# Seven-product pairs of a gated MLP: a raw buffer pool for one quarter of the weights, and matmuls held to the order in which the kernel writes them

## The chip, the cores and the metric

The kernel runs on one core of one Trainium2 chip. The metric is device time in microseconds (us): the median of several executions. A profile is one further execution, recorded by the hardware profiler; its span runs from the first to the last recorded instruction, and its own time is a little longer than its span. The engines are called PE (matrix multiply), PEld (its weight loads), DVE (vector), ACT (scalar), POOL (general) and SP (which here only issues transfers).

## The reference

One decoder layer over 512 tokens of width 1024, in float32: a combined input projection, block-sparse causal attention and a causal mean-pool mixer in parallel, gates, an output projection, a layer norm, and then a gated MLP with a causal width-3 convolution, followed by a second layer norm. The part that matters here is the MLP's input projection:

```python
a, u = jnp.split(h @ w_ffn_in[l], 2, axis=-1)     # h: (512, 1024), each half: (512, 2816)
a = causal_dwconv(a, conv_w[l], conv_b[l])
f = (jax.nn.gelu(a, approximate=False) * u) @ w_ffn_out[l]
h = layer_norm(ALPHA * h + f, ln2_g[l], ln2_b[l])
```

The 2816 columns of `a` and of `u` are cut into 22 tiles of 128; tile `f` of `a` and tile `f` of `u` make a pair.

## The kernel before

**Number format.** Each float32 operand is split into a rounded part (hi) and a remainder (lo), and a product is three matmuls: hi·hi, hi·lo, lo·hi (`mm3`, lines 182 to 186). For a weight chunk the split costs ACT a copy into `whi` (line 69) and then DVE a subtraction into `wlo` (line 70). A chunk is 128 x 1024 (512 KB) or, for the quarter called D, 128 x 512 (256 KB).

**Stages.** Input projection and attention, branch projections, output projection and first layer norm, MLP input, MLP output (itself done with seven products over a 2 x 2 blocking), second layer norm. All weights pass one list, `chunks`, in order. `weights(i)` runs the list ahead to chunk `i + LEAD` (LEAD is 3) and hands back chunk `i`; `fetch` loads a chunk into a raw buffer (`wraw`, 3 buffers) and splits it into one of 5 `whi` and one of 5 `wlo` buffers (RING).

**Seven-product pairs.** For `f` from 4 to 17 (`SEVEN`), the 2 x 2 scheme is used over the two halves of the reduction (`k1`, `k2`) and the two halves of the tokens (`t1`, `t2`), so that a pair needs seven products of 4 x 3 matmuls with 256 columns in place of eight. Four chunks stand for its weights: A (the `a` tile), X (a sum built in memory: a load of `u` by SP, line 131, on which POOL's accumulating transfer adds `a`, line 132), D (the second half of the `u` tile, loaded by itself) and Y, which is not loaded: two DVE additions make it from X's raw buffer and A's raw buffer (line 144), into a raw buffer of its own. `fetch_seven` (lines 134 to 151) does this; A, D and Y draw on the same three `wraw` buffers, and X has two `xraw` buffers in the pool `xu`. That pool stands where `hraw` (16 KB a partition) stood before. X's load is issued five chunks ahead (`AHEAD`).

`seven(f)` writes its products in this order, each by `s_mm`: A0 (first half of A), X0, then the previous pair's last product Y1 (kept in the list `pending`), Y0, A1, D0, X1. Three banks hold the results: `sa` receives A0, Y0, X1 and Y1 one after the other, `sb` receives X0 and D0, `sc` receives A1. Between them ACT and DVE read partial results out (lines 699 to 711). After Y1, `gated` (lines 621 to 630) does the convolution, the GELU and the product with `u`. In the profile a matmul's operands tell the product: `sa<-hT` is A0 or Y1, `sa<-nT` is Y0 or X1, `sb<-T` is X0 or D0, `sc<-hT` is A1.

**What sets the order.** The kernel is written as one sequence; the compiler's scheduler places each engine's instructions by a modelled timeline. An instruction whose operands the model takes as late is overtaken by a later-written one that it takes as ready. The resulting order of each engine is fixed in the program, and so is the assignment of buffers: a chunk takes a buffer that the model saw come free. On the chip each engine then works through its own list.

## Time and profile before

| what | value |
|---|---|
| runs shown | 651.03, 651.3, 653.6 us; median 651.3 |
| the profiled execution | 649.74 us, of it span 648.0 |
| PE busy | 635.7 us in 3586 matmuls |
| DVE, ACT, POOL busy | 449.5, 328.0, 111.6 us |
| bytes moved | 94.79 MB, mean 146 GB/s |
| granted clock of PE | 0.996 of full, mean |
| seven-product stage | 347.95 us (first A0) to about 500 us (last Y1), 1176 matmuls of 256 columns |

The 40-slice rows of the page give each engine's busy share in tenths. A matmul's recorded duration overlaps the next one's, so the distance from one matmul's start to the next is what tells of lost time: 0.12 us for 256 columns.

### The profile page before, as it was taken

The page shows a single profiled execution, that of the slowest core. Times are in us where ns is not written, and L with a number is a line of the kernel's source. Part 1 is how long each engine was busy: PE and PEld are TensorE (multiplying, and loading weights), DVE is VectorE, ACT ScalarE, POOL GpSimd, SP SyncE. Part 2 cuts the span into 40 slices and gives each one's busy share as a digit, 9 for nine tenths or more (in the row PEclk, how much of TensorE's full clock was granted, in tenths as well). Part 3 has the DMA queues.
Part 4 walks back from the last instruction along what each step waited for, and adds up shares of the span by engine and source line. Part 5 has one row for each costly group of instructions (what it writes and reads, how often), then busy time and mean ns, then how long its engine had stood idle before and what let it go on. Part 6 is the DMA issues. An engine that isn't in the chain of part 4 may idle for free.

```text
span 648.0 us, 9322 instructions
## 1 busy us (share of the span) xinstructions
PE 635.7 (98%) x3586; PEld 551.4 (85%) x3586; DVE 449.5 (69%) x666; ACT 328.0 (51%) x475; POOL 111.6 (17%) x153
## 2 busy tenths in 40 slices
PE   9999999999999999999999999999999999999994
PEld 6888787877888888888999999998998888888884
DVE  6466665564532576299667888787986859698596
ACT  6547556675522333215444556455665337465452
POOL 1605361211000123300010101010100201123302
PEclk9999999999999999999999999999999999999998
DMA  9643222212222227404056686677635895989905
GB/s 323 197 166 99 82 81 82 74 67 89 74 95 98 91 98 286 136 1 162 2 150 173 170 208 155 179 179 188 165 128 163 274 264 137 218 188 193 282 4 129
DMA packets 32540, 94.79 MB, mean 146 GB/s; under 512 B 3688, under 2 KB 3944, under 8 KB 32240
## 3 DMA queue, kind: packets, MB, share of 16 engines
q1 hardware_dynamic: 22832, 66.91, 30.4%
q0 software_dynamic: 9088, 26.24, 20.7%
q10 hardware_dynamic: 576, 1.05, 0.5%
q8 instruction: 28, 0.46, 0.3%
q14 instruction: 16, 0.13, 0.1%
HBM read 91.02 MB, written 3.17 MB: 145 GB/s over the span
## 4 chain that ended last, share of the span: by engine, by line
PE 91%; DVE 3%; POOL 2%; DMA 1%; ACT 1%; issue 1%; DVEq 0%; ACTq 0%; POOLq 0%
PE fi L186 5%; PE fi L184 5%; PE fi L185 5%; PE g L184 5%; PE g L186 4%; PE g L185 4%; PE sa L184 4%; PE sa L186 4%; PE sa L185 4%; PE v L285 3%; PE wo L186 2%; PE br L186 2%; PE br L184 2%; PE wo L184 2%; PE wo L185 2%; PE br L185 2%
## 5 line engine op out<-in xcount | busy, mean ns | idle before, releaser
L70 DVE TENSOR_TENSOR wlo<-wraw,whi 128x1024 fp32r<-128x1024 f32 (+1 forms) x119 | 144.1, 1214 | 59.2 <-ACT whi L69 57.7
L69 ACT ACTIVATE whi<-wraw 128x1024 fp32r<-128x1024 f32 (+1 forms) x118 | 117.2, 996 | 131.9 <-PE g L185 23.6
L186 PE MATMUL fi<-hT_hi,wlo 128*128 128x512 f32 (+1 forms) x168 | 56.7, 339 | 0.0
L185 PE MATMUL fi<-hT_lo,whi 128*128 128x512 f32 (+1 forms) x168 | 56.7, 339 | 0.0
L184 PE MATMUL fi<-hT_hi,whi 128*128 128x512 f32 (+1 forms) x168 | 56.4, 340 | 0.0
L184 PE MATMUL g<-xT_hi,whi 128*128 128x512 f32 x128 | 50.3, 393 | 0.0
L186 PE MATMUL g<-xT_hi,wlo 128*128 128x512 f32 x128 | 49.9, 390 | 0.0
L185 PE MATMUL g<-xT_lo,whi 128*128 128x512 f32 x128 | 49.8, 389 | 0.0
L132 POOL DMA_DIRECT2D xraw<-in_w_fi x14 | 17.0, 1215 | 183.7 <-DVE y L624 70.2
L69 ACT ACTIVATE whi<-tw 128x1024 fp32r<-128x1024 f32 (+1 forms) x30 | 29.4, 982 | 21.6 <-DMA tw<-in_w_fo 8.1
L70 DVE TENSOR_TENSOR wlo<-tw,whi 128x1024 fp32r<-128x1024 f32 (+1 forms) x30 | 33.3, 1127 | 8.4 <-ACT whi L69 8.4
L185 PEld LDWEIGHTS fi<-hT_lo,whi 128*128 128x128 f32 x168 | 31.9, 190 | 3.5
L186 PEld LDWEIGHTS fi<-hT_hi,wlo 128*128 128x128 f32 x168 | 31.9, 190 | 3.3
L184 PEld LDWEIGHTS fi<-hT_hi,whi 128*128 128x128 f32 x168 | 31.6, 190 | 3.3
L184 PE MATMUL sa<-hT_hi,whi 128*128 128x256 f32 x112 | 31.9, 285 | 2.0 <-ACT whi L69 1.9
L186 PE MATMUL sa<-hT_hi,wlo 128*128 128x256 f32 x112 | 31.7, 284 | 0.0
L185 PE MATMUL sa<-hT_lo,whi 128*128 128x256 f32 x112 | 31.6, 283 | 0.0
L184 PE MATMUL sb<-T_hi,whi 128*128 128x256 f32 x112 | 31.5, 282 | 0.0
L184 PE MATMUL sa<-nT_hi,whi 128*128 128x256 f32 x112 | 31.5, 281 | 0.0
L186 PE MATMUL sa<-nT_hi,wlo 128*128 128x256 f32 x112 | 31.3, 279 | 0.0
L185 PE MATMUL sa<-nT_lo,whi 128*128 128x256 f32 x112 | 31.3, 279 | 0.0
L185 PE MATMUL sb<-T_lo,whi 128*128 128x256 f32 x112 | 31.3, 279 | 0.0
(250 smaller groups left out, 1762.8 us busy)
## 6 DMA issues: line engine op xcount, KB each, us to landing
wraw<-in_w_fi SPq DMA_DIRECT2D x30, 512.0 KB, 3.6
wraw<-in_w_c SPq DMA_DIRECT2D x28, 512.0 KB, 3.4
tw<-in_w_fo POOLq DMA_DIRECT2D x20, 512.0 KB, 8.3
xraw<-in_w_fi SPq DMA_DIRECT2D x14, 512.0 KB, 4.9
xraw<-in_w_fi POOLq DMA_DIRECT2D x14, 512.0 KB, 5.7
wraw<-in_w_fo SPq DMA_DIRECT2D x10, 512.0 KB, 5.1
tw<-in_w_fo SPq DMA_DIRECT2D x10, 512.0 KB, 6.6
wraw<-in_w_br SPq DMA_DIRECT2D x8, 512.0 KB, 3.3
```

What stands on the lines that cost most here:

```text
L69: nc.scalar.activation(hi, src, AF.Copy)
L70: nc.vector.tensor_tensor(lo, src, hi.bitcast(F32), op=ALU.subtract)
L132: nc.gpsimd.dma_start(v, bass.AP(tensor=a.tensor, offset=a.offset, ap=[[pst, pn], [u.offset + S - a.offset, 2], [est, S]]), accum_op=ALU.add)
L184: nc.tensor.matmul(out_, wh, ah, start=start, stop=False, **kw)
L185: nc.tensor.matmul(out_, wh, al, start=False, stop=False, **kw)
L186: nc.tensor.matmul(out_, wl, ah, start=False, stop=stop, **kw)
L285: nc.tensor.matmul(bs[j], xs_[j][a], (wh, wl)[b], start=kt == 0 and n == 0, stop=False)
```

## The change

D gets raw buffers of its own: two tiles `draw` of 128 x 512 in the pool `xu`; `wraw`, still three buffers, serves A and Y alone in these pairs. The list `pending` is created early, since `fi_mm` now reads it. `mm3` takes a function `pin`, applied to each of its three matmuls. `s_mm` passes `tc.keep_in_program_order`, and `fi_mm` (the plain tiles) passes it while a Y1 is pending, which is so for one tile, the first after pair 17. That function adds a scheduling edge to the instruction written just before on the same engine: the pinned matmul is placed behind it. It adds no semaphore wait. All matmuls of the 14 pairs therefore stand in PE's list in the order in which `seven` writes them.

```diff
@@ -120,6 +120,7 @@
     raws = {}
+    pending = []
     sums = list(SEVEN)
     xu = None
@@ -136,8 +137,10 @@
         n = S if q == "D" else D
         if q == "X":
             raw = raws[f, "X"]
-        else:
-            raw = raws[f, q] = wp.tile([P, D], F32, tag="wraw", name=f"wraw{i}", bufs=3)[:, :n]
+        elif q == "D":
+            raw = xu.tile([P, S], F32, tag="draw", name=f"draw{f}", bufs=2)
+        else:
+            raw = raws[f, q] = wp.tile([P, D], F32, tag="wraw", name=f"wraw{i}", bufs=3)
@@ -179,11 +182,11 @@
-    def mm3(out_, w, a, start, stop, **kw):
+    def mm3(out_, w, a, start, stop, pin=lambda ins: ins, **kw):
         (wh, wl), (ah, al) = w, a
-        nc.tensor.matmul(out_, wh, ah, start=start, stop=False, **kw)
-        nc.tensor.matmul(out_, wh, al, start=False, stop=False, **kw)
-        nc.tensor.matmul(out_, wl, ah, start=False, stop=stop, **kw)
+        pin(nc.tensor.matmul(out_, wh, ah, start=start, stop=False, **kw))
+        pin(nc.tensor.matmul(out_, wh, al, start=False, stop=False, **kw))
+        pin(nc.tensor.matmul(out_, wl, ah, start=False, stop=stop, **kw))
@@ -616,7 +619,8 @@
         for kt in range(KT):
-            mm3(b[:, t], (wh[:, kt, :], wl[:, kt, :]), (hT_hi[:, kt, t], hT_lo[:, kt, t]), kt == 0, kt == KT - 1)
+            mm3(b[:, t], (wh[:, kt, :], wl[:, kt, :]), (hT_hi[:, kt, t], hT_lo[:, kt, t]), kt == 0, kt == KT - 1,
+                tc.keep_in_program_order if pending else lambda ins: ins)
@@ -679,13 +683,11 @@
-    pending = []
-
     def s_mm(f, q, part, act_, b, start, skip=True):
         wh, wl = split3(weights(fi_at[f, q]), 4 if q == "D" else KT)
         for k in range(4):
             mm3(b, (wh[:, 4 * part + k, :], wl[:, 4 * part + k, :]), (act_[0][:, k, :], act_[1][:, k, :]),
-                start and k == 0, k == 3, skip_group_check=not start)
+                start and k == 0, k == 3, tc.keep_in_program_order, skip_group_check=not start)
```

## The prediction

> **What bounds the kernel now.** I read the page's busy shares and slices first, then PE's waits, then the work by stretches, then PE's rows around each gap.

> ```profile
> span 648.0 us, 9322 instructions
> PE 635.7 (98%) x3586; PEld 551.4 (85%) x3586; DVE 449.5 (69%) x666; ACT 328.0 (51%) x475; POOL 111.6 (17%) x153
> PEclk9999999999999999999999999999999999999998
> ```

> ```profile
> PE sa L184 <- ACT whi L69: 1.9, 2, 1.1
> ```

> PE is busy 635.7 of 648.0 us at a granted clock that stays full up to the tail, and the whole seven-product stage shows it idle for 1.9 us, in two waits, both of an `sa` product for ACT's copy of a weight chunk. The stretches below (busy us and count of PE, PEld, DVE, ACT, POOL; clock; DMA share; GB/s) say where.

> ```profile
> 348.00:362.00 14.00, 14.00 (x120) 14.00 (x119) 10.75 (x15) 7.10 (x11) 2.16 (x2) 1.00 0.54 136
> 365.00:400.00 35.00, 35.00 (x296) 35.00 (x296) 29.31 (x43) 20.06 (x30) 3.61 (x3) 1.00 0.75 196
> 400.00:412.00 12.00, 11.15 (x93) 10.80 (x91) 10.67 (x15) 7.49 (x12) 2.41 (x2) 1.00 0.58 157
> 439.00:447.00 8.00, 6.81 (x54) 6.37 (x53) 6.95 (x11) 5.37 (x7) 1.20 (x1) 1.00 0.69 150
> 505.00:570.00 65.00, 65.00 (x288) 53.84 (x287) 48.87 (x52) 32.53 (x38) 10.39 (x12) 1.00 0.85 222
> 348.00:485.00 137.00, 134.96 (x1128) 134.14 (x1127) 114.09 (x159) 78.77 (x118) 14.20 (x12) 1.00 0.65 167
> ```

> In the undisturbed stretches PE starts a 256-column matmul every 0.1185 us (35.00 us for some 295), full to the brim. Everything that this change can win lies in two short stretches, around 400 to 412 and 439 to 447. DVE is at 114.09 of 137 us (83%) and ACT at 78.77 (57%): neither bounds the stage by itself, but DVE has only 17% to spare. After 505 PE is full again at 222 GB/s.

> **The change, part by part.** First the most it can give. Idle time as the waits view counts it starts only when the modelled end of a matmul has passed, so I go by starts.

> ```profile
> 400.77 0.39 PE L184 MATMUL sa<-nT_hi,whi 128*128 128x256 f32 x1
> 401.12 0.39 PE L184 MATMUL sb<-T_hi,whi 128*128 128x256 f32 x1
> 410.84 0.28 PE L186 MATMUL sb<-T_hi,wlo 128*128 128x256 f32 x1
> 411.97 0.39 PE L184 MATMUL sa<-hT_hi,whi 128*128 128x256 f32 x1 [0.85 <-ACT whi L69]
> 412.19 0.28 PE L185 MATMUL sa<-hT_lo,whi 128*128 128x256 f32 x1
> 441.98 0.28 PE L186 MATMUL sc<-hT_hi,wlo 128*128 128x256 f32 x1
> 443.34 0.39 PE L184 MATMUL sa<-hT_hi,whi 128*128 128x256 f32 x1 [1.08 <-ACT whi L69]
> 443.56 0.28 PE L185 MATMUL sa<-hT_lo,whi 128*128 128x256 f32 x1
> 443.95 0.39 PE L184 MATMUL sa<-hT_hi,whi 128*128 128x256 f32 x1
> ```

> Against 0.12 us: 410.84 to 411.97 loses 1.01, 441.98 to 443.34 loses 1.24, 443.56 to 443.95 loses 0.27. Each matmul of 0.39 us (five here, one more at 446.69) holds the next back by a further 0.10 us, 0.6 in all. Four small delays (0.05 at 400.60, 0.03, 0.04, 0.08 elsewhere) make 0.2. Together 3.3 us of 648.0, 0.5%. That is the ceiling: the number and the shape of the matmuls do not change.

> D's own buffers. The first stall hangs on a transfer, as the chain of work shows:

> ```profile
> 403.58 0.68 DVE wraw L144
> 404.28 1.74 DVE wlo L70 x2
> 406.03 4.74 DMA wraw<-in_w_fi
> 410.86 1.07 ACT whi L69
> 411.97 0.39 PE sa L184
> ```

> A's load left only when the Y additions and a split had freed a raw buffer (406.03), took 4.74 us, and PE stood waiting for its copy. Three buffers hold A, D, Y, so the next A waits for this pair's Y. With D elsewhere, the next A takes the buffer of the Y before, freed about a pair (9.9 us) earlier. SP's own waits say that this is the common case:

> ```profile
> SPq L146 <- DVE wlo L70: 43.5, 13, 6.3
> SPq L146 <- DVE wraw L144: 27.6, 5, 7.5
> ```

> Between 348 and 485 us these are 18 waits, up to 7.5 us each. A's load can leave several us earlier, against the 0.85 us by which it was late: I count the whole first group (1.14 us at 410 to 412) as gone. Cost: no instruction is added. 14 loads of 256 KB leave earlier on SP and behind each stands the next X load; they wait on `draw` instead of `wraw`, released by a split one pair earlier. The pool `xu` grows into the rest of `hraw`'s place, so the first D load can wait for the last reader of `hraw`, as the first X load already does (328.54); its split runs at 341.48, so some 10 us cover it.

> ```profile
> 328.54 14.69 SPq L131 DMA_DIRECT2D xraw<-in_w_fi  x3
> 341.48 0.61 ACT L69 ACTIVATE whi<-wraw 128x512 fp32r<-128x512 f32 x1
> ```

> The pins. The second stall is not a transfer's but one of order. D's copy (128 x 512) stood at the head of ACT's queue, idle for 3.88 us, until PE gave a `whi` buffer back; the other copies and DVE's splits stood behind it and came in a bunch, which the chain of work follows up to PE:

> ```profile
> 439.35 0.63 ACT L69 ACTIVATE whi<-wraw 128x512 fp32r<-128x512 f32 x1 [3.88 <-PE sa L185]
> ```

> ```profile
> 440.02 0.69 DVE wlo L70
> 442.34 1.22 DVE wlo L70
> 443.95 0.39 PE sa L184
> ```

> With PE in the written order, releases of the 5 `whi` buffers come at an even beat: after Y1, A1, D0, X1, each 12 x 0.1185 = 1.42 us long. I follow the buffers: A of a pair takes the one that Y1 freed and has 4 products' time to be split in, X takes A's (3 products, 4.27 us), D takes D's (6), Y takes X's (A0, X0, Y1 in between: 3, 4.27 us). What such a turn costs is seen for a Y:

> ```profile
> 357.82 0.28 PE L186 MATMUL sa<-nT_hi,wlo 128*128 128x256 f32 x1
> 358.01 1.06 ACT L69 ACTIVATE whi<-wraw 128x1024 fp32r<-128x1024 f32 x1 [0.91 <-PE sa L185]
> 359.11 1.23 DVE L70 TENSOR_TENSOR wlo<-wraw,whi 128x1024 fp32r<-128x1024 f32 x1
> ```

> From 357.94 (the X1 done) to 360.34 is 2.40 us, so 1.87 us are over in the tightest turns. If that cover goes, each us beyond it is a us of PE, since nothing may overtake now: behind a late Y0 stand A1, D0, X1, and ACT and DVE wait for those banks. In the trace PE did otherwise: at 350.80 it ran A1 and put Y0 behind it.

> ```profile
> 350.80 0.29 PE L184 MATMUL sc<-hT_hi,whi 128*128 128x256 f32 x1
> 351.49 0.37 ACT L699 ACTIVATE y<-sa 128x256 f32<-128x256 f32 x1
> 352.24 0.28 PE L184 MATMUL sa<-nT_hi,whi 128*128 128x256 f32 x1
> ```

> For the first pair, which has no Y1 between, Y0 pinned at 350.80 needs ACT's read of `sa`, done at 351.86 there: up to 1.1 us lost once, or nothing if ACT, no longer held by a copy of the late next A, reads when A0 is done (350.80 less the 1.42 us of X0). I take 0.3, nearer to nothing, since A's load is the part that comes earlier. For the other 13 pairs the price of new waits lies between 0 and, if all cover failed, the rival below; I take 0, by the 2.40 against 4.27. Pinning the one plain tile after pair 17 costs nothing: its operands are as ready as those of the tile behind it.

> The rate itself: PE's spacing stays 0.1185 by the rows, in the unmixed stretch 348 to 362 (118 starts in 14.00 us) as in the mixed one 365 to 400, so the sum takes no gain from unmixing. [...]

> Sum: span 648.0 - 3.3 + 0.3 = 645.0, and with the 1.7 us around it (649.74 - 648.0) 646.7 for the profiled execution. That execution lies 1.6 us below the median of the runs shown, 651.3; the same 3.0 us off that median gives 648.3. What is late next is nothing in this stage; after 505 PE is full, with the weight loads at 85% of DMA.

> **The rivals.**

> *Y stands late at the head (slower).* The Y additions (2 x 0.69) and another chunk's split (1.23) may fall into Y's turn: 2.40 + 1.38 + 1.23 = 5.01 against 4.27, 0.74 us a pair, 9.6 us over 13 pairs, less the 3.3: 657.6. It decides from 1.87 us of other DVE or ACT work ahead of Y's split. For it: DVE at 83%, and the scheduler itself ran A1 ahead of Y0, so its model took Y for late. Against it: Y's first addition ran at 403.58, ahead of the splits from 404.28 on, and DVE's 17% is 1.7 us a pair. [...]

> *Only the transfer is cured.* The order around 441 comes from splits on DVE and copies on ACT, and a similar knot may form again (1.7 us at 441 to 444, 0.2 nearby): -1.4, so 649.9. For it: the 3.88 us before 439.35 were a wait for PE, which a raw buffer does not touch. Against it: the pins change exactly those releases.

> *The gain is given back.* PE reaches the plain tiles 3 us earlier, their weights and the first pieces of the output weights share a DMA at 85%, and PE waits there: 651.3. Against it: PE shows no wait at all from 447 on.

> *The order sets the spacing.* Within one unbroken product at 481.40 to 482.53, ten starts lie 0.113 us apart; were this due to order, 1176 x 0.0055 = 6.5 us more: 641.8. The stretch 348 to 362, equally unbroken at 0.1185, is against it.

> ```profile
> 481.40 0.28 PE L186 MATMUL sb<-T_hi,wlo 128*128 128x256 f32 x1
> 482.53 0.28 PE L186 MATMUL sc<-hT_hi,wlo 128*128 128x256 f32 x1
> ```

> **How the numbers follow.** Likeliest, 0.44: 648.3, own range 647.3 to 649.4. Transfer alone, 0.16: 649.9. Given back, 0.12: 651.3. Y late, 0.26: 652 (where a few pairs stall) to 661, worked out as 657.6 for all of them. Spacing, 0.02: 641.8. About what a measurement can tell from no change is 0.5%, 3.26 us, so faster means below 648.04: half of the likeliest case, whose ceiling is the 3.3 us, the last case and a little scatter, 0.28. Slower, above 654.6, is the Y case where most pairs stall, 0.20. Within: 0.52. The range leaves out 0.05 below and 0.13 above: 647.2 to 657.0.

> **What would show it.** Right: in the profile after, `sa`, `sb`, `sc` products in runs of exactly 12; PE's wait for `whi` at 0 to 0.3 us; the stage from the first A0 to the last X1 shorter by 3 us; SP's `wraw` waits in the stage well below the 71 us of the two rows above. Wrong: an `sa<-nT` product waiting in pair after pair for DVE's `wlo` or ACT's `whi` (Y late), or waits of plain `fi` or `fo` tiles after 500 (given back). The sum fails first where I followed the buffers: another assignment than the one I took from the order of releases would shrink a turn from 4.27 us to 2.85, which 2.40 barely fits.

## The result and the profile after

The changed kernel takes 695.65 us (693.98 to 697.6, four runs) against 651.22 (651.03 to 653.6, four runs): a ratio of 1.0674, interval 1.0633 to 1.0716. It is 6.7% slower; 648.3 had been predicted, and at most 657.0. The profiled execution took 693.98 us, 692.3 of it span.

The page of the changed kernel (busy shares, and the slices of PE and of its granted clock):

```profile
span 692.3 us, 9323 instructions
PE 654.9 (95%) x3586; PEld 567.5 (82%) x3586; DVE 446.5 (65%) x666; ACT 327.8 (47%) x475; POOL 111.1 (16%) x153
PE   9999999999999999999997987798789999999995
PEclk9999999999999999999997999898979999999998
```

Work and instruction counts are as before. PE now has holes in the seven-product stage, and after some of them the granted clock falls to 0.50 (its mean is 0.969, in the kernel before 0.996). PE's waits in the changed kernel (us in total, times, longest):

```profile
PE sa L187 <- DVE sa L713: 18.2, 11, 3.0
PE sb L189 <- DVE wlo L70: 9.1, 7, 3.7
```

All waits of the stage are for DVE: for X's `wlo` at X0, and for the third addition of the pair before (line 713, 711 in the old numbering: y and the bank `sc` into the bank `sa`), without which Y1 may not write that bank. Counted by starts as in the prediction, the waits come to 31.8 us, and matmuls that started 0.21 us apart instead of 0.12 to another 14.6. The stage up to the last Y1 lasts 193.3 us in place of 151.6; seven fewer of the plain matmuls stand inside it (7 x 0.23 = 1.6 us), so it lost 43 of the 44 us.

At the first hole, PE's rows:

```profile
369.01 0.28 PE L188 MATMUL sb<-T_lo,whi 128*128 128x256 f32 x1
372.99 0.58 PE L189 MATMUL sb<-T_hi,wlo 128*128 128x256 f32 x1 [3.69 <-DVE wlo L70]
376.33 0.58 PE L187 MATMUL sa<-hT_hi,whi 128*128 128x256 f32 x1 [0.84 <-DVE sa L713]
```

DVE's rows in the same place, and the two halves of X's transfer on SP and POOL:

```profile
357.89 0.38 SPq L132 DMA_DIRECT2D xraw<-in_w_fi  x1
362.64 1.21 POOL L133 DMA_DIRECT2D xraw<-in_w_fi  x1 [12.26 <-DMA xraw<-in_w_fi]
369.85 0.69 DVE L147 TENSOR_TENSOR wraw<-xraw,wraw 128x512 f32<-128x512 f32 x1 [5.03 <-DMA xraw<-in_w_fi]
370.46 0.74 DVE L629 SCALAR_TENSOR_TENSOR y<-sa,cvp,y 128x510 f32<-128x510 f32 x1
371.12 0.68 DVE L147 TENSOR_TENSOR wraw<-wraw,wraw 128x512 f32<-128x512 f32 x1
371.72 1.22 DVE L70 TENSOR_TENSOR wlo<-xraw,whi 128x1024 fp32r<-128x1024 f32 x1
374.72 1.21 DVE L70 TENSOR_TENSOR wlo<-wraw,whi 128x1024 fp32r<-128x1024 f32 x1
375.85 0.42 DVE L713 TENSOR_TENSOR sa<-y,sc 128x256 f32<-128x256 f32 x1
```

DVE stands still for 5.03 us before an addition of Y, until X has landed. That X and that Y are of pair 7. Behind the addition waits X's split of pair 6, whose copy ACT had finished at 365.76 and which PE needs at 369.1. The order is in the program. The following lines are from the program's list for DVE in the changed kernel, not from the profile, with places in the list ahead and the buffers numbered (the number behind `xraw` is the pair; of each pair the first addition and the split of X):

```
313 L147 TensorTensor wraw63_3099<-xraw5_2884,wraw60_3014 128x512
321 L147 TensorTensor wraw67_3224<-xraw6_3011,wraw64_3122 128x512
323 L70 TensorTensor wlo61_3034<-xraw5_2884,whi61_3033 128x1024
331 L147 TensorTensor wraw71_3349<-xraw7_3119,wraw68_3247 128x512
334 L70 TensorTensor wlo65_3159<-xraw6_3011,whi65_3158 128x1024
```

The additions of pair f+1 (321, 331) stand ahead of the split of pair f (323, 334), for 12 of 13 neighbours; in the kernel before, for none. That closes a loop. X has two buffers, so X of pair f+2 can load only when X of pair f has been split; the additions of pair f+2 wait for that load and its accumulation; and the split of pair f+1 stands behind them. At this place the split of X5 ended at 357.86, X7 landed 11.9 us later, and the additions, the y instruction between them and the split of X6 followed until 372.93: 15.1 us from one split to the next, where 12 x 7 matmuls at 0.1185 need 9.95. At the next place the transfer took 10.2 us; over the stage the splits are 13.86 us apart on average. From pair 6 to pair 17 every first addition starts 0.08 us after the landing of its X, and DVE has stood still for 1.1 to 5.0 us before it, 26.9 us in all.

What opened the way is the raw buffer: with D elsewhere, Y's own raw buffer is free about a pair earlier, and the model that orders the instructions put the additions there. That is read from the lists of the variants below: D on the shared buffers, no early addition; D on its own, early additions.

### The profile page after: what moved, and what is told of

It reads as the page before. It is cut to its first block, busy times and chain, and to the rows that moved or that the text cites. A ratio compares the mean times of both kernels' runs of the same rounds, so it can differ in the third digit from the quotient of the medians.

```text
span 692.3 us, 9323 instructions
## 1 busy us (share of the span) xinstructions
PE 654.9 (95%) x3586; PEld 567.5 (82%) x3586; DVE 446.5 (65%) x666; ACT 327.8 (47%) x475; POOL 111.1 (16%) x153
## 5 line engine op out<-in xcount | busy, mean ns | idle before, releaser
L70 DVE TENSOR_TENSOR wlo<-wraw,whi 128x1024 fp32r<-128x1024 f32 (+1 forms) x105 | 134.4, 1283 | 93.5 <-ACT whi L69 93.0
L69 ACT ACTIVATE whi<-wraw 128x1024 fp32r<-128x1024 f32 (+1 forms) x104 | 108.2, 1043 | 141.3 <-PE sa L188 40.9
L187 PE MATMUL sa<-hT_hi,whi 128*128 128x256 f32 x112 | 36.1, 322 | 18.2 <-DVE sa L713 18.2
L189 PE MATMUL sb<-T_hi,wlo 128*128 128x256 f32 x112 | 32.6, 291 | 9.1 <-DVE wlo L70 9.1
L187 PEld LDWEIGHTS sa<-hT_hi,whi 128*128 128x128 f32 x112 | 24.1, 215 | 20.7 <-DVE sa L713 20.5
L69 ACT ACTIVATE whi<-tw 128x1024 fp32r<-128x1024 f32 (+1 forms) x30 | 29.4, 983 | 21.1 <-DMA tw<-in_w_fo 7.5
L70 DVE TENSOR_TENSOR wlo<-tw,whi 128x1024 fp32r<-128x1024 f32 (+1 forms) x30 | 33.3, 1126 | 7.8 <-ACT whi L69 7.8
L189 PE MATMUL sa<-hT_hi,wlo 128*128 128x256 f32 x112 | 34.7, 309 | 0.0
L188 PE MATMUL sa<-hT_lo,whi 128*128 128x256 f32 x112 | 34.6, 309 | 0.0
L187 PE MATMUL sa<-nT_hi,whi 128*128 128x256 f32 x112 | 34.2, 306 | 0.0
L188 PE MATMUL sa<-nT_lo,whi 128*128 128x256 f32 x112 | 34.0, 304 | 0.0
L189 PE MATMUL sa<-nT_hi,wlo 128*128 128x256 f32 x112 | 33.9, 303 | 0.0
```

The source lines that it names most:

```text
L69: nc.scalar.activation(hi, src, AF.Copy)
L70: nc.vector.tensor_tensor(lo, src, hi.bitcast(F32), op=ALU.subtract)
L187: pin(nc.tensor.matmul(out_, wh, ah, start=start, stop=False, **kw))
L188: pin(nc.tensor.matmul(out_, wh, al, start=False, stop=False, **kw))
L189: pin(nc.tensor.matmul(out_, wl, ah, start=False, stop=stop, **kw))
```

## The experiments

Theory L is the loop. Rival P is that the pins themselves hold PE back. The table anticipates the measurements. Pace is the mean distance from one X split to the next between pairs 5 and 16; the last three columns are the trace's times of one loop: the end of the split of X6, which frees the buffer, the landing of X8 in it, and the start of the first addition of Y8. (With three buffers X8 follows X5 and lands before the split of X6.) The kernel before ran beside each set of variants, with medians from 650.46 to 651.22; the ratios are to the run beside.

| variant | median, us | ratio to before (95%) | pace, us | X6 split | X8 landed | Y8 addition |
|---|---|---|---|---|---|---|
| before | 651.22 | 1 | 10.26 | 364.63 | 375.78 | 381.30 |
| changed | 695.65 | 1.0674 (1.0633 to 1.0716) | 13.86 | 372.93 | 383.08 | 383.16 |
| D's buffers alone | 664.75 | 1.0207 (1.0173 to 1.0241) | 11.14 | 370.99 | 382.41 | 382.49 |
| pins alone | 653.18 | 1.0035 (1.0024 to 1.0047) | 10.27 | 367.81 | 378.73 | 381.25 |
| additions behind the X split | 675.55 | 1.0359 (1.0314 to 1.0404) | 11.82 | 367.14 | 378.98 | 379.00 |
| three X buffers | 661.27 | 1.0171 (1.0151 to 1.0192) | 11.07 | 366.97 | 366.56 | 374.87 |
| no accumulating transfer | 662.38 | 1.0158 (1.0128 to 1.0188) | 11.24 | 369.38 | 373.86 | 377.29 |
| additions late | 651.84 | 1.0016 (1.0002 to 1.0030) | 10.27 | 366.30 | 377.97 | 379.73 |
| pins, DVE ordered | 648.39 | 0.9969 (0.9957 to 0.9981) | 9.99 | 367.25 | 378.28 | 380.75 |
| both, DVE ordered | 647.93 | 0.9957 (0.9945 to 0.9969) | 9.99 | 366.95 | 379.22 | 380.32 |
| buffers, DVE ordered, no pins | 647.78 | 0.9958 (0.9942 to 0.9974) | 10.07 | 364.95 | 375.64 | 380.64 |

**The two halves of the change.** D back on `wraw` with the pins kept, and D's buffers kept with the pins taken out:

```diff
-        elif q == "D":
-            raw = xu.tile([P, S], F32, tag="draw", name=f"draw{f}", bufs=2)
...
```

> The pins alone: D goes back to the shared raw buffers, all matmuls of the pairs stay in the written order. Theory L (a loop through DVE: with D in buffers of its own, Y's raw buffer is free a pair earlier, DVE's list puts Y's first addition of pair f+1 ahead of the split of X of pair f, and DVE then stands still until X of pair f+1 has landed): here the list of DVE has every X split ahead of the next pair's addition, so the loss is gone, 647.5 to 650 us, and no long wait of DVE for X's transfer. Rival P (the pins themselves: PE held in order stands behind late operands in pair after pair): the loss stays, 685 to 700 us.

```diff
-                start and k == 0, k == 3, tc.keep_in_program_order, skip_group_check=not start)
+                start and k == 0, k == 3, skip_group_check=not start)
...
```

> D's own raw buffers alone, nothing pinned. Theory L: DVE's list has the addition ahead of the split before it in 3 pairs (6, 7 and 12), where the changed kernel has 12; at some 44.4/12 = 3.7 us each up to 11 us, 653 to 662 us, and DVE's waits for X's transfer at those three places only. Rival P (the pins are the cause): 649 to 652 us.

The pins alone cost 0.35%, the buffers alone 2.1%. Rival P falls as the cause of the 44 us. L was right in kind and off in size on both: the pins alone are 3 us above its range, the buffers alone 3 above theirs. In the latter the list has an early addition at three pairs (6, 7 and 12), yet DVE waits for X at pairs 8 and 13 too, since there the addition stands right behind the split. And at eight pairs, 12 and seven without an early addition, it waits for the load of A and not for X:

```profile
DVE wraw L147 <- DMA xraw<-in_w_fi: 16.0, 4, 4.9
DVE wraw L147 <- DMA wraw<-in_w_fi: 15.2, 8, 3.7
```

So with D's buffers alone the loss is not the loop through X alone (4.6 us of the first row are the first pair's, ahead of the stage); why A's loads were late there stays open. Together the halves cost far more than their sum (0.35 + 2.1 against 6.7%): early additions in 3 pairs when PE's list may be mixed, in 12 when it may not.

**The addition behind the split.** An edge puts Y's additions of pair f behind X's split of pair f-1:

```diff
+                if f - 1 in xsplit:
+                    tc.add_manual_dep(add.ins, xsplit[f - 1].ins.name, ..., reason="Y behind X")
```

> Both parts of the change, and one scheduling edge more: Y's two additions of pair f stand behind the split of X of pair f-1 in DVE's list. Theory L: the loop is open, PE in the written order has no stall to speak of, 647.5 to 650 us. Rival P: 685 to 700 us, as with the pins.

675.55: neither. The swap is gone from the list and 20 us with it, but not the other 24. DVE's rows of this variant show the first addition waiting directly behind the split, and the third addition (line 719 here) behind both additions and Y's split:

```profile
377.31 1.23 DVE L70 TENSOR_TENSOR wlo<-xraw,whi 128x1024 fp32r<-128x1024 f32 x1 [0.19 <-ACT whi L69]
379.00 0.69 DVE L148 TENSOR_TENSOR wraw<-xraw,wraw 128x512 f32<-128x512 f32 x1 [0.47 <-DMA xraw<-in_w_fi]
383.21 0.43 DVE L719 TENSOR_TENSOR sa<-y,sc 128x256 f32<-128x256 f32 x1
```

DVE's waits for X in the stage and PE's for the third addition:

```profile
DVE wraw L148 <- DMA xraw<-in_w_fi: 2.4, 4, 0.9
PE sa L193 <- DVE sa L719: 18.2, 12, 2.3
```

The wait for X is thus the small part here, four pairs. Most of the 24 us is the third addition: where X had landed in time (at pair 14 by 0.25 us, the addition following the split without a gap), PE still lost 1.3 us to it, since Y's second addition and Y's split stand between line 718 and line 719 in 12 pairs.

For the wait, the theory had to be put more exactly: what counts is how long after the split of pair f the additions of pair f+2 come up in DVE's list, against the 10 to 12 us that the transfer takes. Where they come up sooner DVE waits for the landing, whether the next split is behind them or ahead. At the table's place the addition starts within 0.1 us of the landing in the changed kernel, with D's buffers alone and here, 10.2, 11.5 and 11.9 us after the split; with the pins alone it comes 13.4 us after the split and 2.5 after the landing, in the kernel before 16.7 and 5.5.

**Opening the loop without touching DVE's order.** First with three X buffers, for which one buffer each of D and u was given up:

```diff
-        x_ = raws[f, "X"] = xu.tile([P, D], F32, tag="xraw", name=f"xraw{f}", bufs=2)
+        x_ = raws[f, "X"] = xu.tile([P, D], F32, tag="xraw", name=f"xraw{f}", bufs=3)
...
-            raw = xu.tile([P, S], F32, tag="draw", name=f"draw{f}", bufs=2)
+            raw = xu.tile([P, S], F32, tag="draw", name=f"draw{f}", bufs=1)
...
-        u = xu.tile([P, S], F32, tag="u", name=f"u{f}", bufs=2)
+        u = xu.tile([P, S], F32, tag="u", name=f"u{f}", bufs=1)
```

> Both parts of the change with three buffers for X in place of two (to make room, one buffer for D and one for u in place of two each). DVE's list still has Y's addition ahead of the X split before it in the same 12 pairs. Theory L: X's load leaves a pair earlier, so it has landed when the addition comes up; DVE's wait for X's transfer falls from 1 to 5 us a pair to under 0.5, and the time to 648 to 656 us (single buffers for D and u may cost a little). If the order of DVE itself, and not the wait for X's transfer, were the cause, or the pins were: 685 to 700 us.

733.6 us (ratio 1.1269, 1.1235 to 1.1303), and it decides nothing: the single buffer for u took over as the limit, as PE's waits in this variant say.

```profile
PE sb L187 <- ACT u L703: 52.9, 13, 4.8
```

The same with both u buffers, the room found in the tile of the warm-up matmuls and a gap in the memory's layout, and with one buffer for D:

```diff
-        x_ = raws[f, "X"] = xu.tile([P, D], F32, tag="xraw", name=f"xraw{f}", bufs=2)
+        x_ = raws[f, "X"] = xu.tile([P, D], F32, tag="xraw", name=f"xraw{f}", bufs=3)
...
-            raw = xu.tile([P, S], F32, tag="draw", name=f"draw{f}", bufs=2)
+            raw = xu.tile([P, S], F32, tag="draw", name=f"draw{f}", bufs=1)
...
-    warm = const.tile([P, S], mybir.dt.bfloat16, name="warm")
+    warm = const.tile([P, P], mybir.dt.bfloat16, name="warm")
...
-        nc.tensor.matmul(wb_, warm[:, :P], warm, start=True, stop=True)
+        for j in range(4):
+            nc.tensor.matmul(wb_[:, j * P:(j + 1) * P], warm, warm, start=True, stop=True)
...
-    sp.tile([P, 48], F32, name="sp_gap")
```

> Both parts of the change, with three buffers for X instead of two and both buffers for u kept (one buffer for D, a smaller warm-up tile and a dropped gap tile make the room; the warm-up issues 128-column matmuls). DVE's list still has Y's addition ahead of the X split of the pair before in the same 12 pairs. Theory L (the loop from X's split over the freed buffer, the load, the accumulating transfer and the addition back to the next X split): a third buffer lets X leave a pair earlier, DVE's waits for X's transfer fall from 1 to 5 us a pair to under 0.3, 650 to 658 us. Rival P or any cause in DVE's order alone: 685 to 700 us.

And the changed kernel without POOL's half of the transfer:

```diff
-        nc.gpsimd.dma_start(v, bass.AP(tensor=a.tensor, offset=a.offset,
-                                       ap=[[pst, pn], [u.offset + S - a.offset, 2], [est, S]]), accum_op=ALU.add)
```

> Both parts of the change, without POOL's accumulating transfer: X holds the u tile alone, so the a tile is left out of the sums X and Y, and the output is another. DVE's list keeps the early additions in the same 12 pairs. Theory L: X has landed some 6 us earlier, DVE does not wait for it, and what is left is what the run with three X buffers had left, the third addition standing behind Y's additions and X's split: 655 to 664 us. If the early place in DVE's list cost the time without the transfer: 685 us and more.

661.27 and 662.38: two ways to have X landed in time, the same 33 to 34 us gained, with the early additions still in the list. (The former lies 3 us above L's range; the latter's trace is of its slowest execution, 668.35 us.) From pair 5 on DVE does not wait for X in either trace. That settles the loop as the larger part of the loss. What remains, 11 us, is the third addition; with three X buffers it is PE's only wait in the stage:

```profile
PE sa L187 <- DVE sa L713: 9.4, 11, 1.8
```

Eleven pairs, 0.8 us by starts in nine of them: Y's two additions (0.69 each), out of place, and the splits of X and Y push the third addition past the point where Y1 begins.

**The additions late.** Both parts of the change, the additions behind the third addition of pair f-2, where the pins alone have them (`behind_add` adds such an edge behind the third addition of the pair that it is given):

```diff
+                behind_add(nc.vector.tensor_tensor(raw[:, c], o, a[:, c], op=ALU.add), f - 2)
...
```

> Both parts of the change, and an edge that puts Y's two additions of pair f behind the third addition (u and y with the banks) of pair f-2, which is where the kernel with the pins alone has them. Theory L with the correction from the run with the edge behind X's split (what counts is how long after the split two pairs before the addition stands, against some 12 us of load and accumulation): 652 to 655 us, as with the pins alone. If D's own buffers cost something besides the early addition: over 658 us.

651.84, 0.2 us under the range expected, and the loss is accounted for. PE still waits in it as with the pins alone, whose rows show why (DVE, then PE):

```profile
399.82 0.42 DVE L710 TENSOR_TENSOR u<-u,sa 128x256 f32<-128x256 f32 x1
400.16 1.22 DVE L757 TENSOR_TENSOR ra<-fT 128x1024 f32<-128x1024 f32 x1
401.29 1.22 DVE L70 TENSOR_TENSOR wlo<-wraw,whi 128x1024 fp32r<-128x1024 f32 x1
402.43 0.42 DVE L711 TENSOR_TENSOR sa<-y,sc 128x256 f32<-128x256 f32 x1
401.55 0.28 PE L187 MATMUL sb<-T_hi,wlo 128*128 128x256 f32 x1
402.90 0.39 PE L185 MATMUL sa<-hT_hi,whi 128*128 128x256 f32 x1 [1.08 <-DVE sa L711]
```

The third addition was ready at 400.2, with line 710 done, and ran 2.2 us later: the next pair's Y split stands ahead of it in 12 of the 14 pairs, and in two of these a sum that belongs to the output stage too. Y1 waits.

**DVE put in order.** Y's split of pair f behind the third addition of pair f-1, and the output stage's sums kept at their written place; once with the pins alone, once with both parts and late additions, once with the latter and no pins:

```diff
+        if q == "Y":
+            behind_add(last, f - 1)
...
-            nc.vector.tensor_tensor(rd(c), side(0, c, t1), side(0, c, t2), op=ALU.subtract)
+            tc.keep_in_program_order(nc.vector.tensor_tensor(rd(c), side(0, c, t1), side(0, c, t2), op=ALU.subtract))
...
```

> The pins alone, and two edges on DVE: Y's split of pair f stands behind the third addition of pair f-1, and the six sums for the output stage that the scheduler had drawn into this stage stay at their written place. Theory (in the pins-alone run PE waits for that third addition because a split of 1.22 us, and in two pairs a sum of 1.22 us as well, stands ahead of it): the 2 x 1.24 us and the twice 0.1 us in each of 13 pairs go, some 4.5 us, so 648 to 650 us; PE's wait for the third addition is gone. If something else held it: 652 to 654 us as before.

> Both parts of the change, with the additions behind the third addition of pair f-2 as well as the two edges of the run before. If the raw buffers bring anything once the additions stand late (the loads of A and D leave earlier): 0.3 to 1 us less than with the shared buffers, 647 to 649.5 us. If they bring nothing: the same within 0.3 us.

> The best kernel so far without the pins: D's own raw buffers, the additions behind the third addition of pair f-2, Y's split behind that of pair f-1, the output stage's sums at their written place. If the order of DVE alone makes the stage free of stalls: 647.5 to 649 us, like the pinned one. If PE's written order is needed for it (the scheduler still mixes products, which moves the releases of the weight buffers): 650 to 660 us, with PE waiting in several pairs.

648.39, 647.93 and 647.78. The second, by stretch (columns as in the prediction), has no hole, and its DVE rows have the third addition right behind line 720 and Y's additions 13.4 us after the split two pairs before:

```profile
349.00:485.00 136.00, 136.00 (x1146) 136.00 (x1145) 111.08 (x155) 80.05 (x122) 13.67 (x12) 1.00 0.66 167
```

```profile
378.39 0.41 DVE L720 TENSOR_TENSOR u<-u,sa 128x256 f32<-128x256 f32 x1
378.84 0.43 DVE L721 TENSOR_TENSOR sa<-y,sc 128x256 f32<-128x256 f32 x1
379.18 1.22 DVE L70 TENSOR_TENSOR wlo<-wraw,whi 128x1024 fp32r<-128x1024 f32 x1
380.32 0.68 DVE L148 TENSOR_TENSOR wraw<-xraw,wraw 128x512 f32<-128x512 f32 x1
```

All three beat the kernel before by 0.3 to 0.4%. D's own buffers bring at most a little: 0.46 us between the first two medians, less than their intervals tell apart, though the first pair's wait (below) is only in the first. And the third expectation's fear was wrong: without the pins PE's list is mixed again, and the stage has no wait either. The pins are not needed for the gain; the order on DVE is. Whether it would do as much with neither part of the change, and which of its two edges does how much, was not run.

## Why the prediction was wrong, step by step

- **The ceiling of 3.3 us: right.** With no wait left in the stage the kernel is 2.8 us faster (647.93 against 650.71), close to the 648.3 that was forecast for it, but the change as made does not get there.
- **"D's own buffers. Cost: no instruction is added": the step that failed.** It followed the freed buffer to A's load alone. The same buffer frees Y's additions, and these are instructions in DVE's list, ordered by a model. The prediction listed SP's and PE's queues and left out what the change would move on DVE. Measured: 0 in the sum, 44 us on the chip, 33 to 34 of them the loop through X's two buffers.
- **X's transfer was never followed as a loop.** The split frees the buffer, and load and accumulation land 10 to 12 us later. In the kernel before, from pair 5 on, the addition came 4.1 to 8.0 us behind the landing (5.0 for pair 7, 5.5 for pair 8). That slack could have been read there.
- **"Behind a late Y0 stand A1, D0, X1": the wrong turn was watched.** Neither Y nor the `whi` buffers became late; X0 and Y1 did, X0 for its split, Y1 for the third addition. The window of 2.85 us from X1's end to Y1's start, in which DVE must do lines 710 and 711, was tighter than the 4.27 that were worked out. With the pins alone it is missed by 0.1 us in most pairs and 1.24 in two.
- **The rival "Y stands late at the head"** had the right sign and engine, and its bound of 9.6 us was far too small, since it counted work ahead of an instruction and not a wait for a transfer ahead of it. Its argument against, that the additions ran early, was upside down: early is what hurt.
- **The first pair, 0 to 1.1 us: right.** With the pins alone its Y0 waits 0.9 us (1.1 with DVE ordered); with both parts and late additions 0.27, and nothing with DVE ordered too. The 0.3 taken was for the right reason, A's earlier load, but by another way than the one given: with the pins alone DVE's first addition of Y5 waits 1.36 us for A's load, the convolution and the GELU stand behind it, and ACT's read of `sa` behind the GELU.
- **"The gain is given back" and "the order sets the spacing": not seen.** The stage after costs the same within 1.6 us in every variant but one (a single wait of 0.5 to 1.0 us stands in it in some); without the accumulating transfer it costs 2.4 us more, with two waits. The unbroken runs of 12 keep 0.118 to 0.120 us in the median.
- **The clock** was taken as full throughout. A third of the loss, 14 us, is matmuls at half of it.
- **The signs named for being right** came true but for the stage's length: the products stand in 98 runs of exactly 12, PE never waits for `whi` in the stage, and SP's waits ahead of the loads of A and D are 29.0 us there, well below 71. The sign of "Y late" did not appear. The same view of SP has what none of them watched: ahead of X's loads SP waits 117.6 us, in the kernel before 25.0.

## What to carry to other kernels

A raw buffer that came free about a pair earlier let the scheduler move DVE's additions ahead in 12 pairs; before counting what a change to buffers brings, list on every engine each instruction whose earliest time it moves, and what would then stand behind it in that engine's list. For an instruction that waits for a transfer, measure the distance from the event that starts the transfer to the instruction in the old trace and compare it with the transfer's time: that slack, here 4.1 to 8.0 us, is what a reordering may use up. And when an engine is 98% busy, an order edge on the engine that feeds it may be worth more than one on itself: here 653.18 us with edges on PE alone, 648.39 with edges on DVE as well.

## What the runs showed of the hardware

PE's granted clock fell to half after some of the holes and not after others. Stretches of the changed kernel, a hole and what follows (the clock is the third number from the right):

```profile
413.20:418.40 5.20, 1.91 (x14) 1.50 (x13) 5.17 (x8) 1.29 (x3) 0.00 (x0) 1.00 0.55 169
418.40:424.00 5.60, 5.58 (x47) 5.58 (x48) 1.89 (x2) 3.06 (x4) 1.20 (x1) 1.00 0.83 170
439.60:445.00 5.40, 1.87 (x14) 1.46 (x12) 5.37 (x9) 2.23 (x4) 0.00 (x0) 0.91 0.36 97
445.00:451.00 6.00, 5.98 (x28) 5.98 (x29) 1.89 (x2) 2.11 (x3) 1.20 (x1) 0.52 0.86 196
```

```profile
416.68:420.10 3.42, 1.68 (x14) 1.68 (x15) 1.69 (x3) 0.07 (x1) 1.20 (x1) 1.00 0.75 262
440.57:443.99 3.42, 1.44 (x10) 1.24 (x10) 3.42 (x6) 1.45 (x4) 0.00 (x0) 1.00 0.32 90
443.99:447.40 3.41, 2.38 (x11) 2.38 (x12) 0.98 (x2) 0.21 (x1) 0.92 (x1) 0.50 0.89 275
```

The first hole falls on two steps of the grid, and each keeps 1.68 us or more of PE's work; of the second, one step has only 1.44, and the clock is half from its end on. Over these two traces, each of the 8 steps at full clock with 1.53 us of PE's work or less was followed by half clock, and none of the 367 with 1.68 us or more was. Full clock came back after each of the six steps at half clock with 3.29 us of work or more, and after none of the seven with 2.81 or less. Why the clock keeps such a grid the traces do not show.
